# A transformer layer on one core: the second expert matrix split whole for seven experts, first rows by one-hot products, a later evacuation

## The chip, the cores and the metric

The kernel runs on one core of a Trainium2 chip. The metric is the device time in microseconds (us) of the whole program; the median of several runs is compared. The engines are TensorE (PE: matmuls; PEld its weight loads), VectorE (DVE), ScalarE (ACT), GpSimd (POOL) and SyncE (SP), each with its own queue of instructions, in which it works strictly in order; transfers run on 16 DMA engines.

## The reference

One decoder layer in fp32, 1024 tokens of width 1024: a modulated norm, one projection into the queries, keys and values of two attention kinds, the attentions, an output projection with a gated residual; then a second modulated norm, a router, and 32 experts of which each token takes four.

```
    x = x + gate1 * mixed
    h2 = rms_norm(x, norm2_g) * (1.0 + scale2) + shift2
    logits = h2 @ w_router + b_router
    top_val, top_idx = lax.top_k(logits, 4); gates = softmax(top_val)
    # for each expert e, over the rows xe that chose it:
        gu = xe @ w_gate_up[e] + b_gate_up[e]          # 1024 x 2048
        g = min(gu[:, :1024], 7);  u = clip(gu[:, 1024:], -7, 7)
        y = ((u + 1) * g * sigmoid(1.702 * g)) @ w_down[e] + b_down[e]
    return x + gate2 * sum over a token's experts of gate * y
```

An expert's two matrices are 12 MB in fp32, read once each: 384 MB in all.

## The kernel before

Four stages follow each other: the projections, the attentions, then eight row blocks of 128 tokens (output projection, norm, router), then the 32 experts.

**The row blocks** (class `Block`). Block by block the kernel computes x1 (`products`, `add`), the norm's factor (POOL takes a power, line 111, from `rsqrt_start`), the rows h2 (`rows_start`, `rows_out`, which writes them to the DRAM buffer `h2d`), the router's logits and the four choices (`logits`), each row's place within its experts (`places`), and a table row per choice: `scattered` issues four indirect DMAs on POOL, line 982, from `pay` (token and gate) to the places `sli` in the DRAM table `tab`. Before that, `places` lets POOL write the token numbers into `pay` (line 944). `pay` and `sli` come from a pool with three buffers, and the last block has its own. For the expert that is done first, the rows' list is also kept on chip: `hot` is a one-hot matrix (token by place), `tg` holds token, gate and a one, and `listed` adds hot's product with tg for each block into the PSUM tile `p0` (line 960); after the last block DVE makes the list `slots0` of it, POOL gathers the rows from `h2d` (line 1146), and PE transposes them (line 1174).

**The experts.** An order by rank is computed from the counts of rows. An expert at a position works with a fixed number of columns C, its capacity: 172, 136, 200, 128, 136, 128, 188, ... down to 96 (rows above it go through a loop at the end). Up to 128 rows are one row block, above that there are two. An expert's weights are 12 chunks of 1 MB. Ten of them are split into a high part (ACT, line 826, two halves a chunk, `hb`) and a low part in bf16 (DVE, line 813, `ha`); the activations are split likewise (`xx`, `xb`). `products` then takes four columns blocks of 128 at once: 32 matmuls of the high weights with high and low activations side by side (line 1196, max(256, 2C) columns), and 32 of the low weights with the activations in bf16 (line 1202, C columns). Chunks 8 and 9, the first half of the down matrix's columns, are not split: `expert` multiplies them as plain fp32 (line 1252, 32 matmuls that the profile shows as 64 records), from two buffers of their own (`draw`). The other chunks go through a ring of six (`eraw`).

In the plain product ACT evacuates a pair of output blocks to `yl` (line 1263) as soon as it is finished: blocks 0 and 1 before PE has done 2 and 3. The transposes of the next expert's rows (`between`, that is `stage_t`, line 1174) stand after each half of it. PSUM has four tiles of two banks in rotation (`banks`).

What starts when is written by hand: PE, ACT, DVE and SP execute in program order. `done()` is called at 14 places of an expert; the table TG says up to which of the 20 halves splits may then have been issued (`pump`), and `pump` also issues every chunk load for which a buffer is free. NH = 12 halves may be split ahead. The chunk loads stand on SP's queue, gathers and scatters on POOL's.

## Time and profile before

| | |
|---|---|
| median of 3 runs | 2157.39 us (2155.97 to 2163.31) |
| the profiled execution | 2155.82 us, span 2154.0 us |
| PE, PEld | 2046.7 us (95%), 1914.8 us (89%) |
| DVE, ACT, POOL | 1631.7 (76%), 1357.8 (63%), 481.7 us (22%) |
| DMA | 549.53 MB, mean 255 GB/s |
| first product of the first expert starts | 745.96 us |

The span runs from the first to the last instruction of the profiled execution. A share of busy time is a mean over the four stages; the section of rows below therefore cuts the span by windows. Idle time of an engine is put down to what came last of the things it waited for.

### The profile page before, as it was taken

What the parts mean: (1) busy time and instruction counts of PE and PEld (TensorE: products, weight loads), DVE (VectorE), ACT (ScalarE), POOL (GpSimd) and SP (SyncE); (2) the same over time, 40 slices, a digit from 0 to 9 for tenths busy, and PEclk for the clock granted to TensorE, in tenths of its full rate; (3) what the DMA queues carried; (4) which work ended last, traced back from release to release, by engine and by line L of the source; (5) the groups of instructions that cost most, each with busy time, mean ns of one, the idle gap of its engine ahead of it and who ended that gap; (6) DMA issues with size and microseconds to landing.
All of it is one profiled execution on the core that took longest, in us unless ns stands there. A gap on an engine that the chain in (4) does not pass through costs nothing.

```text
span 2154.0 us, 43837 instructions
## 1 busy us (share of the span) xinstructions
PE 2046.7 (95%) x16922; PEld 1914.8 (89%) x16922; DVE 1631.7 (76%) x2838; ACT 1357.8 (63%) x2391; POOL 481.7 (22%) x466
## 2 busy tenths in 40 slices
PE   6999999999999699999999999999999999999997
PEld 6877778998887599999998999999999999999996
DVE  6587765776666778788787877878878878878884
ACT  3522314777643367677677677777877777768774
POOL 2245532111013411112111222112111211211211
PEclk9999999999999799999999999999999999999998
DMA  8267886442233498899799999989999999999993
GB/s 296 67 161 220 217 237 164 112 114 70 90 129 145 158 338 293 268 337 343 268 295 347 289 315 317 324 296 349 309 321 300 355 319 330 325 332 322 332 321 81
DMA packets 273655, 549.53 MB, mean 255 GB/s; under 512 B 31796, under 2 KB 31812, under 8 KB 273316
## 3 DMA queue, kind: packets, MB, share of 16 engines
q1 hardware_dynamic: 251507, 490.61, 67.4%
q0 software_dynamic: 21936, 56.09, 11.2%
q8 instruction: 134, 2.20, 0.4%
q14 instruction: 78, 0.63, 0.1%
HBM read 501.84 MB, written 44.78 MB: 254 GB/s over the span
## 4 chain that ended last, share of the span: by engine, by line
PE 61%; ACT 5%; DMA 3%; DVE 3%; issue 2%; POOL 1%; POOLq 0%; SPq 0%; ACTq 0%; DVEq 0%
PE gu L1196 30%; PE gu L1202 13%; PE gu L1252 10%; PE gu L1285 2%; ACT hb L826 2%; PE gu L1174 2%; PE po L605 1%; ACT yl L1263 1%; DMA eraw<-in_w_down_dram 1%; DMA eraw<-in_w_gate_up_dram 1%; PE pss L567 1%; DMA tab<-pay,sli 1%; PE pt L598 1%; POOL tab L982 1%; DVE ha L813 0%
## 5 line engine op out<-in xcount | busy, mean ns | idle before, releaser
L813 DVE TENSOR_TENSOR ha<-eraw,hb 128x1024 bf16<-128x1024 f32 x640 | 760.0, 1240 | 7.7 <-ACT hb L826 7.7
L826 ACT ACTIVATE hb<-eraw 128x1024 fp32r<-128x1024 f32 x640 | 634.1, 1050 | 21.2 <-DMA eraw<-in_w_down_dram 15.3
L1196 PE MATMUL gu<-xx,hb 128*128 128x256 f32 (+13 forms) x4096 | 586.3, 299 | 2.2 <-DVE xx L1178 2.2
L1196 PEld LDWEIGHTS gu<-xx,hb 128*128 128x128 f32 x4096 | 552.9, 189 | 2.6 <-DVE xx L1178 2.4
L1202 PEld LDWEIGHTS <-ha 128*128 128x128 bf16 x5120 | 310.6, 97 | 11.8 <-issue 1.5
L1252 PE MATMUL gu<-ay,draw 128*128 128x128 f32 (+19 forms) x2048 | 277.9, 292 | 36.4 <-ACT yl L1263 32.9
L1252 PEld LDWEIGHTS gu<-ay,draw 128*128 128x128 f32 x2048 | 260.5, 192 | 44.5 <-ACT yl L1263 39.7
L1202 PE MATMUL gu<-xb,ha 128*128 128x128 bf16 (+19 forms) x4096 | 271.6, 224 | 0.0
L1216 ACT ACTIVATE tb<-gu,bcol 128x128 f32<-128x128 f32 (+19 forms) x512 | 156.9, 369 | 89.8 <-PE gu L1202 80.8
L1182 POOL DMA_INDIRECT out_dram<-y,slot x47 | 79.7, 1695 | 404.9 <-ACT y L1286 263.0
L1146 POOL DMA_INDIRECT xg<-h2d,slot x47 | 65.9, 1401 | 393.0 <-PE gu L1174 86.8
L1196 PE MATMUL gu<-ax,hb 128*128 128x256 f32 (+13 forms) x1024 | 144.5, 298 | 0.0
L1276 ACT ACTIVATE tb<-gu,bcol,g2c 128x128 f32<-128x128 f32 (+19 forms) x128 | 56.3, 465 | 132.4 <-PE gu L1202 104.8
L1196 PEld LDWEIGHTS gu<-ax,hb 128*128 128x128 f32 x1024 | 137.4, 188 | 0.6
L571 DVE CUSTOM_DVE_ANT_0 p<-pss,bias 128x1024 f32<-128x1024 f32 (+7 forms) x128 | 94.4, 755 | 52.1 <-ACT p L580 23.5
L1277 DVE SCALAR_TENSOR_TENSOR ay<-gu,g2c,tb 128x128 f32<-128x128 f32 (+19 forms) x128 | 46.2, 362 | 113.9 <-ACT tb L1276 113.9
L1258 POOL CAST ab<-ax 128x512 bf16<-128x512 f32 (+19 forms) x64 | 69.7, 1094 | 263.7 <-ACT ax L1256 263.7
L605 PE MATMUL po<-vsb,pT 128*128 128x64 f32 (+1 forms) x864 | 111.3, 275 | 2.9 <-ACT pT L599 1.4
L605 PEld LDWEIGHTS po<-vsb,pT 128*128 128x128 f32 x864 | 105.4, 194 | 5.8 <-ACT pT L599 2.0
L580 ACT ACTIVATE p<-p,mn 128x1024 f32<-128x1024 f32 (+7 forms) x128 | 98.6, 773 | 11.9 <-DVE mn L571 11.2
L111 POOL TENSOR_TENSOR rrs<-vrs,nhalf 128x8 f32<-128x8 f32 (+2 forms) x48 | 66.1, 1377 | 169.6 <-DVE vrs L109 167.8
L459 PE MATMUL pp<-wh,hb 128*128 128x512 f32 x240 | 100.5, 419 | 0.0
(275 smaller groups left out, 3080.6 us busy)
## 6 DMA issues: line engine op xcount, KB each, us to landing
eraw<-in_w_gate_up_dram SPq DMA_DIRECT2D x256, 1024.0 KB
draw<-in_w_down_dram SPq DMA_DIRECT2D x64, 1024.0 KB
eraw<-in_w_down_dram SPq DMA_DIRECT2D x64, 1024.0 KB
wraw<-in_w_ada_dram SPq DMA_DIRECT2D x32, 512.0 KB
wraw<-in_w_in_dram SPq DMA_DIRECT2D x23, 512.0 KB
hb<-in_w_ada_dram SPq DMA_DIRECT2D x16, 512.0 KB
qd<-tt POOLq DMA_DIRECT2D x32, 256.0 KB, 3.7
kd<-tt POOLq DMA_DIRECT2D x32, 256.0 KB, 4.0
```

Of the source, the lines that this page charges most:

```text
L459: nc.tensor.matmul(pp, hh[b][:, k], wh[:, kk], start=(k == 0), stop=False)
L571: nc.vector.tensor_tensor_reduce(p[:, :n], pss[:, :n], bias[:, (NB - 1 - ib) * P:(NB - 1 - ib) * P + n], -1.0, 3.0e38, OP.add, OP.min, mn)
L580: nc.scalar.activation(p, p, AF.Exp, bias=self.mn[c], scale=-1.0, accum_out=self.l[:, c:c + 1])
L605: nc.tensor.matmul(self.po[:, :w], self.pT[:, k], vsb[self.br][:, k, self.h * w:(self.h + 1) * w], start=(k == 0), stop=(k == self.ib))
L813: nc.vector.tensor_tensor(parts[t][1], raws[c][:, 2 * q:2 * q + 2], parts[t][0].bitcast(F32), OP.subtract)
L826: nc.scalar.activation(h_, raws[c][:, 2 * q:2 * q + 2], AF.Copy)
L1182: nc.gpsimd.indirect_dma_start(out=out, out_offset=bass.IndirectOffsetOnAxis(ap=sl.bitcast(I32)[:n, 0:1], axis=0), in_=y[:n], in_offset=No ...
L1196: nc.tensor.matmul(pg[j // 2][:, j % 2, :max(256, 2 * C)], w[k][0][:, j * P:(j + 1) * P], xk[k], start=(k == 0), stop=False)
L1202: nc.tensor.matmul(pg[j // 2][:, j % 2, C:2 * C], w[k][1][:, j * P:(j + 1) * P], xb[:, k], start=False, stop=(k == KT - 1))
L1216: nc.scalar.activation(t[:, j], p[:, j, C:2 * C], AF.Identity, bias=bc[:, f + j:f + j + 1], scale=1.0)
L1252: nc.tensor.matmul(place(j), raw[:, k, j * P:(j + 1) * P], a[:, 4 * kh + k], start=(kh + k + j % 2 == 0), stop=(kh == 1 and k == 3 and j % ...
L1258: nc.gpsimd.tensor_copy(ab[:, f], ah[:, f, :C].bitcast(F32))
```

## The change

Constants CWH = 164 and a second table TGW of twelve entries are new. The parts:

- **Whole split.** The seven experts with C of 164 or more (172, 200, 188, 180, 172, 168, 164, at positions 0, 2, 6, 10, 14, 18, 22) split chunks 8 and 9 too; all their 12 chunks go through the ring of six, 24 halves. In place of the plain product stands a third kind of call of `products`, with the two halves of the next rows' transposes in its middle (`mid`), and the evacuation of the split products (`outgoing`). Their activations are split by two column blocks (`activations(f, 2)`), after each pair of `a`, instead of by four.
- **Late evacuation.** In the other 25 experts (`plain`) the four yl activations stand behind all 32 matmuls.
- **First rows.** The list of the first expert from blocks 0 to 6 is read after the last block's `add`, and the rows gathered then, into `hb` buffers. The last block's rows don't go through DRAM for this expert: `stage_0` multiplies the gathered rows by the identity and adds the product of the last block's h2 with its one-hot matrix. `listed` of the last block, its list, the order by counts and what hangs on it come after that. Rows of the list that belong to the last block point to zeroed rows of `h2d` in the early gather (one DMA more, in the attention stage).
- **pay and sli** have a buffer for each of the eight blocks.
- The count of overflowing rows is read into registers at position 5 instead of after the last expert.

```diff
+CWH = 164
+TGW = (12, 14, 16, 18, 19, 21, 23, 24, 26, 30, 31, 36)
...
+                nc.sync.dma_start(h2d[S - P:S, :], z)
...
+            whole = [CAPS[r] >= CWH for r in seq]
+            splits = [(i * NCH + c, q) for i in range(E) for c in range(NCH) if whole[i] or c not in PLAIN for q in range(2)]
...
-                return "p" if d % NCH in PLAIN else "s"
+                return "p" if d % NCH in PLAIN and not whole[d // NCH] else "s"
...
-                    pay = (sm if self.b < NB - 1 else rt).tile([P, TOPK, 2], F32, name="pay")
+                    pay = rt.tile([P, TOPK, 2], F32, name="pay", bufs=NB)
...
-                    self.sli = (sm if self.b < NB - 1 else rt).tile([P, TOPK], I32, name="sli")
+                    self.sli = rt.tile([P, TOPK], I32, name="sli", bufs=NB)
...
-            cur.add(1)
-            pv.listed()
+            early = [rt.tile([P, 2], F32, name=f"early{i}") for i in range(len(BLOCKS0))]
+
+            def fetch_list():
+                nc.vector.tensor_copy(sums0, p0[:, :3 * len(BLOCKS0)])
+                slots_of(sums0, early)
+
+            cur.add(1, fetch_list)
+            xg0 = []
+            for (t0, n), sl in zip(BLOCKS0, early):
+                xg0.append(slot(False).bitcast(F32))
+                nc.gpsimd.indirect_dma_start(out=xg0[-1][:n], out_offset=None, in_=h2d,
+                                             in_offset=bass.IndirectOffsetOnAxis(ap=sl.bitcast(I32)[:n, 0:1], axis=0))
...
+        def stage_0(st):
+
+            st["x"] = operand(C0, "xx", "xb")
+            bc = st["bc"]
+            nc.vector.tensor_mul(bc[:, 2 * KT:], bc[:, 2 * KT:], g2c)
+            pts = [banks().rearrange("p g (k c) -> p (g k) c", k=4) for _ in BLOCKS0]
+            for (t0, n), xg, pt in zip(BLOCKS0, xg0, pts):
+                for k in range(KT):
+                    nc.tensor.matmul(pt[:, k, :n], xg[:n, k * P:(k + 1) * P], ident[:n, :n], start=(k % 4 == 0), stop=False)
+            for (t0, n), pt in zip(BLOCKS0, pts):
+                for k in range(KT):
+                    nc.tensor.matmul(pt[:, k, :n], cur.h2[:, k * P:(k + 1) * P], cur.hot[:, t0:t0 + n],
+                                     start=False, stop=(k % 4 == 3))
+                operand_of(st, t0, n, pt)
...
-                    for k in range(4 * kh, 4 * kh + 4):
-                        nc.tensor.matmul(pg[j // 2][:, j % 2, :max(256, 2 * C)], w[k][0][:, j * P:(j + 1) * P], xk[k],
-                                         start=(k == 0), stop=False)
+                for j, k in [(j, 4 * kh + q + r) for q in ((0, 2) if kh and mid else (0,)) for j in range(4)
+                             for r in range(2 if kh and mid else 4)]:
+                    nc.tensor.matmul(pg[j // 2][:, j % 2, :max(256, 2 * C)], w[k][0][:, j * P:(j + 1) * P], xk[k],
+                                     start=(k == 0), stop=False)
                 if kh == 0:
                     done(high=2)
+                    if mid:
+                        low_products(range(4), range(4))
+                        mid()
+            low_products(range(4), range(4 if mid else 0, KT))
...
+        def plain(C, a, bc, d0, activations, between):
...
+                    if j == 1:
+                        activations(4 * kh, 4)
+                        done()
+                if kh:
+                    yl = ap_.tile([P, 4, C], F32, name="yl")
+                    for f in range(4):
+                        nc.scalar.activation(yl[:, f], place(f), AF.Identity,
+                                             bias=bc[:, 2 * KT + f:2 * KT + f + 1], scale=g2c[:, f:f + 1])
...
+                    if whole[i]:
+                        activations(f, 2)
...
-                    if kh and j % 2:
-                        if j == 1:
-                            yl = ap_.tile([P, 4, C], F32, name="yl")
-                        for f in (j - 1, j):
-                            nc.scalar.activation(yl[:, f], place(f), AF.Identity,
-                                                 bias=bc[:, 2 * KT + f:2 * KT + f + 1], scale=g2c[:, f:f + 1])
...
+            if whole[i]:
+                pg = products(C, s_a, t0 + 16, lambda: (between(0), between(1)))
+                yl = ap_.tile([P, 4, C], F32, name="yl")
+                outgoing(yl, pg, 0)
+                done(high=2, low=4)
+            else:
+                yl = plain(C, a, bc, d0, activations, between)
+            pg = products(C, s_a, t0 + (20 if whole[i] else 16))
...
-        st = stage_g(0)
+        st = {"C": C0, "bc": cols.pop(0), "blocks": BLOCKS0, "slots": slots.pop(0)}
+        stage_0(st)
         cur.scattered()
-        stage_t(st, 0)
-        stage_t(st, 1)
...
+            if i == 5:
+                n_over = nc.values_load(tot[0:1, 0:1], min_val=0, max_val=P)
```

Where instructions move, the order of each engine shows it (what an instruction waits for stands in brackets; DMAHW and DMASW are transfers). On PE, the second half of the plain product of the second expert, before: `xg` are the next expert's rows, `ax` the split activations.

```order
L1252 MATMUL gu<-ay,draw 128x136 [waits DMAHW7_49,DVE_49]
L1252 MATMUL gu<-ay,draw 128x136
L1252 MATMUL gu<-ay,draw 128x136 [waits DVE_49]
L1252 MATMUL gu<-ay,draw 128x136 x5
L1252 MATMUL gu<-ay,draw 128x136 [waits Activation_49]
L1252 MATMUL gu<-ay,draw 128x136 x7
L1174 MATMUL gu<-ident,xg 128x128 x4
L1174 MATMUL gu<-ident,xg 128x72 x4
L1196 MATMUL gu<-ax,hb 128x272 [waits DVE_49,PE_49]
```

And the same place after; the plain product's line is now 1241, the transposes' 1171, the split product's 1220.

```order
L1241 MATMUL gu<-ay,draw 128x136 [waits DMAHW0_49,DVE_49]
L1241 MATMUL gu<-ay,draw 128x136
L1241 MATMUL gu<-ay,draw 128x136 [waits DVE_49]
L1241 MATMUL gu<-ay,draw 128x136 x13
L1171 MATMUL gu<-ident,xg 128x128 x4
L1171 MATMUL gu<-ident,xg 128x72 x4
L1220 MATMUL gu<-ax,hb 128x272 [waits DVE_49,PE_49]
```

The wait for ACT within the plain product is gone; the 16 matmuls stand in the same order. On PE ahead of the first expert, before: `tg` and `hot` make the list (line 960), line 1072 counts rows for the order, line 1174 transposes the gathered rows.

```order
L940 MATMUL po<-msk,upper 128x32 [waits DVE_49]
L941 MATMUL po<-mcum,ones 128x32
L960 MATMUL p_6067<-tg,hot 128x3 [waits DVE_49,Pool_49]
L960 MATMUL p_6067<-tg,hot 128x3
L1072 MATMUL po<-mcum,ones 128x32 [waits DVE_49]
L1174 MATMUL gu<-ident,xg 128x128 [waits DMASW2_49,PE_49]
L1174 MATMUL gu<-ident,xg 128x128 x3
L1174 MATMUL gu<-ident,xg 128x44 [waits DMASW3_49,DVE_49]
L1174 MATMUL gu<-ident,xg 128x44 x3
L1174 MATMUL gu<-ident,xg 128x128 x4
L1174 MATMUL gu<-ident,xg 128x44 x4
L1196 MATMUL gu<-xx,hb 128x344 [waits DVE_49]
```

And after; line 1190 multiplies the gathered rows (in `hb` buffers) by the identity, line 1193 the last block's rows by its one-hot matrix.

```order
L954 MATMUL po<-msk,upper 128x32 [waits DVE_49]
L955 MATMUL po<-mcum,ones 128x32
L1190 MATMUL gu<-ident,hb 128x128 [waits DMASW6_49,PE_49]
L1190 MATMUL gu<-ident,hb 128x128 x7
L1190 MATMUL gu<-ident,hb 128x44 [waits DMASW7_49,DVE_49]
L1190 MATMUL gu<-ident,hb 128x44 x7
L1193 MATMUL gu<-hb 128x128 x8
L1193 MATMUL gu<-hb 128x44 x8
L1394 MATMUL gu<-tg,hb 128x3 x2
L1402 MATMUL gu<-mcum,ones 128x32 [waits DVE_49,PE_49]
L1220 MATMUL gu<-xx,hb 128x344 [waits DVE_49]
```

The transposes have become two sets of sixteen matmuls, the list's product and the row count have moved behind them, and the transfers that PE waits for are the early gathers. On POOL around the last block, before: line 111 is the power of the norm, line 982 the table scatters, line 1146 the first expert's gathers.

```order
L982 DMA tab<-pay,sli 36864x2 x4
L111 TENSOR_TENSOR rr_7253<-vr_7251,nhalf 128x1
L982 DMA tab<-pay,sli 36864x2 x4
L111 TENSOR_TENSOR rr_7418<-vr_7416,nhalf 128x1
L982 DMA tab<-pay,sli 36864x2 x4
L1146 DMA xg<-h2d,slots_2975 128x1024
L1146 DMA xg<-h2d,slots_2976 44x1024
L982 DMA tab<-pay,sli 36864x2 x4
L1179 CAST xb<-xx 128x8x128
```

And after; the power is line 113, the scatters line 990, the gathers line 1074.

```order
L990 DMA tab<-pay,sli 36864x2 x4
L113 TENSOR_TENSOR rr_7255<-vr_7253,nhalf 128x1
L990 DMA tab<-pay,sli 36864x2 x4
L1074 DMA hb<-h2d,early_7413 128x1024
L113 TENSOR_TENSOR rr_7429<-vr_7427,nhalf 128x1
L1074 DMA hb<-h2d,early_7414 44x1024
L990 DMA tab<-pay,sli 36864x2 x8
L1180 CAST xb<-xx 128x8x128
L1180 CAST xb<-xx 128x8x44
```

The first gather now stands ahead of the last block's power and the second behind it, both ahead of the last two blocks' scatters.

## Rows read from the trace of the kernel before

**Rows 1.** Windows: length, busy of PE PEld DVE ACT POOL, granted clock, DMA share, GB/s.
```profile
600.00:733.60 133.60, 120.12 (x643) 100.38 (x641) 86.33 (x275) 49.56 (x153) 42.98 (x58) 0.93 0.36 130
733.60:746.00 12.40, 3.77 (x19) 2.73 (x19) 6.50 (x23) 2.80 (x4) 7.04 (x7) 0.50 0.59 191
745.90:1140.00 394.10, 385.73 (x3543) 377.81 (x3544) 315.49 (x452) 279.92 (x439) 67.53 (x56) 1.00 0.91 305
1140.00:2100.00 960.00, 932.79 (x9079) 913.47 (x9078) 788.40 (x1043) 716.16 (x1143) 188.16 (x169) 1.00 0.97 322
```

**Rows 2.** The page, part 5: the lines named in the text.
```profile
L813 DVE TENSOR_TENSOR ha<-eraw,hb 128x1024 bf16<-128x1024 f32 x640 | 760.0, 1240 | 7.7 <-ACT hb L826 7.7
L826 ACT ACTIVATE hb<-eraw 128x1024 fp32r<-128x1024 f32 x640 | 634.1, 1050 | 21.2 <-DMA eraw<-in_w_down_dram 15.3
...
L1252 PE MATMUL gu<-ay,draw 128*128 128x128 f32 (+19 forms) x2048 | 277.9, 292 | 36.4 <-ACT yl L1263 32.9
...
L1277 DVE SCALAR_TENSOR_TENSOR ay<-gu,g2c,tb 128x128 f32<-128x128 f32 (+19 forms) x128 | 46.2, 362 | 113.9 <-ACT tb L1276 113.9
```

**Rows 3.** Waits of PE, 745 to 2130 us: total, times, longest.
```profile
PE gu L1252 <- ACT yl L1263: 32.1, 31, 3.2
```

**Rows 4.** Timeline of PE, second expert: start, length, line, what it waited for.
```profile
830.67 2.12 PE L1252 MATMUL gu<-ay,draw 128*128 128x136 f32 x16 [0.91 <-ACT yl L1263]
832.63 0.85 PE L1174 MATMUL gu<-ident,xg 128*128 128x128 f32 x8
833.28 4.27 PE L1196 MATMUL gu<-ax,hb 128*128 128x272 f32 x32
```

**Rows 5.** Chain of waits, first expert (172 columns): start, length, what.
```profile
770.27 5.10 PE gu L1196 x32
775.37 2.42 PE gu L1202 x32
777.79 4.71 PE gu L1252 x32
...
785.84 0.89 ACT yl L1263 x2
```

**Rows 6.** Chain of waits, third expert (200 columns).
```profile
867.14 5.88 PE gu L1196 x32
873.02 2.76 PE gu L1202 x32
875.78 5.44 PE gu L1252 x32
```

**Rows 7.** Windows, the first expert.
```profile
746.00:797.80 51.80, 50.83 (x401) 49.57 (x402) 40.60 (x48) 34.47 (x52) 10.13 (x8) 0.97 0.93 332
```

**Rows 8.** Waits of all engines, 600 to 735 us.
```profile
POOL pay L944 <- DMA tab<-pay,sli: 10.5, 4, 3.2
...
PE p L960 <- DVE tg L955: 6.2, 5, 2.3
```

**Rows 9.** Timeline of PE ahead of the first expert.
```profile
729.13 0.99 PE L960 MATMUL p<-tg,hot 128*128 128x3 f32 x4 [1.20 <-DVE tg L955]
...
738.03 1.08 PE L1174 MATMUL gu<-ident,xg 128*128 128x128 f32 x4 [4.04 <-DMA xg<-h2d,slots]
741.49 2.25 PE L1174 MATMUL gu<-ident,xg 44*128 44x44 f32 x12 [2.37 <-DMA xg<-h2d,slots]
745.96 1.51 PE L1196 MATMUL gu<-xx,hb 128*128 128x344 f32 x4 [2.22 <-DVE xx L1178]
```

**Rows 10.** Timeline of POOL, the same stretch.
```profile
722.44 0.57 POOL L111 TENSOR_TENSOR rr<-vr,nhalf 128x1 f32<-128x1 f32 x1 [2.17 <-DVE vr L109]
...
732.27 1.02 POOL L1146 DMA_INDIRECT xg<-h2d,slots  x1 [2.11 <-DMA h2d<-h]
733.60 1.66 POOL L1146 DMA_INDIRECT xg<-h2d,slots  x1 [0.31 <-DVE mcum L978]
```

**Rows 11.** Chain of waits, ninth expert.
```profile
1116.45 20.55 DMA eraw<-in_w_down_dram
```

More of the change, by code (lines that the diff above doesn't have):

```diff
@@ L145, in hybrid_layer @@
     PLAIN = (8, 9)
-    SPLIT = [c for c in range(NCH) if c not in PLAIN]
-    NSP = 2 * len(SPLIT)
     tmp.close()
@@ L820, in split_half @@
                 t = at_["split"]
-                c, q = chunk_of(t)
+                c, q = splits[t]
                 h_ = slot(False).rearrange("p (k n) -> p k n", k=2)
@@ L829, in split_half @@
                 at_["split"] += 1
-                if t == E * NSP - 1:
+                if t == len(splits) - 1:
                     low(t)
@@ L1191, in products, with low_products @@
             w = [tuple(q[:, j] for q in parts[t]) for t in range(t0, t0 + 4) for j in range(2)]
-            assert t0 + 3 < at_["split"] - 1 or at_["split"] == E * NSP
+            assert t0 + 3 < at_["split"] - 1 or at_["split"] == len(splits)
+            def low_products(js, ks):
+                for j in js:
+                    for k in ks:
+                        nc.tensor.matmul(pg[j // 2][:, j % 2, C:2 * C], w[k][1][:, j * P:(j + 1) * P], xb[:, k],
+                                         start=False, stop=(k == KT - 1))
@@ L1198, in products @@
                 if kh == 0:
                     done(high=2)
-            for j in range(4):
-                for k in range(KT):
-                    nc.tensor.matmul(pg[j // 2][:, j % 2, C:2 * C], w[k][1][:, j * P:(j + 1) * P], xb[:, k],
-                                     start=False, stop=(k == KT - 1))
-            return pg
+                    if mid:
+                        low_products(range(4), range(4))
+                        mid()
+            low_products(range(4), range(4 if mid else 0, KT))
@@ new lines, in products, with place @@
+            return pg
+        def plain(C, a, bc, d0, activations, between):
+            pg = banks()
+            def place(j):
+                return pg[:, j // 2, j % 2 * 256:j % 2 * 256 + C]
+            for kh in range(2):
+                raw = raws.pop(d0 + kh)
+                for j in range(4):
+                    for k in range(4):
+                        nc.tensor.matmul(place(j), raw[:, k, j * P:(j + 1) * P], a[:, 4 * kh + k],
+                                         start=(kh + k + j % 2 == 0), stop=(kh == 1 and k == 3 and j % 2 == 1))
+                    if j == 1:
[6 more added lines that the diff above has]
+                                             bias=bc[:, 2 * KT + f:2 * KT + f + 1], scale=g2c[:, f:f + 1])
+                freed["p"] += 1
+                done()
+                between(kh)
+            return yl
```

149 lines of the change are left out of this document (73 added, 76 removed).

## The prediction

> **What bounds the kernel now.** I read the windows first, then the waits of TensorE (PE), and last the chain of waits. In the windows [rows 1] the experts' stretch is 1354 us of the 2154.0 us span, and PE is busy for 98% of its first part (385.73 of 394.10) and 97% of its second (932.79 of 960), at the full clock. So a microsecond of PE work or of PE waiting that disappears there is worth up to a microsecond. The same rows hold the warning: the DMA engines' share is 0.91 before 1140 us and 0.97 after it. Weights stream all through the experts, and in the second part only 0.03 of 960, some 29 us, is free on the DMA side. The two earlier stretches look different: 600 to 733.6 us has PE busy 120 of 133.6 us, and in the 12.4 us ahead of the first expert PE works 3.77 us at a granted clock of 0.50, with DMA at 0.59: a stretch of pure latency.
>
> PE's waits inside the experts are nearly one line: L1252 for ACT's yl, 32.1 us in 31 places [rows 3]. The timeline shows one: 0.91 us before the last 16 records of L1252 [rows 4]; the order before has the wait at exactly that matmul. One of the 31 is 3.2 us long; the other thirty average 28.9/30 = 0.96 us, the value used below.
>
> **Late evacuation.** The order after has no ACT wait within the plain product. Thirty waits of 0.96 us, one for the long one and a last one of that kind [the page counts 32.9 in all, rows 2] make about 30 us; I count 31 × 0.96 = 29.8. What hides the evacuation then is PE's next work: eight transposes (0.85 us, rows 4) and the next product's first tile. Four yl activations are 2 × 0.89 = 1.8 us on ACT [rows 5]. The next product uses two of four bank pairs; when the expert after has two row blocks its second tile falls on the plain product's pair and must wait for yl. That tile comes after the transposes and 8 matmuls of 4.27/32 = 0.13 us [rows 4], 1.9 us in all, so the wait is nil when ACT is free and up to one split (1.05 us, rows 2) when one stands ahead in ACT's order. It can happen in 15 of the 25 plain experts: 0 to 16 us. I take 0.25 us each, 4 us, because ACT is busy 716 of 960 us [rows 1] and often isn't free. Sum of this part: 25.8.
>
> **The whole split.** Seven experts replace 64 plain records by a product. At 172 columns a plain half of 32 records is 4.71 us, so 9.42 the pair, and a product is 5.10 + 2.42 = 7.52: 1.90 saved [rows 5]. At 200 columns it is 2 × 5.44 = 10.88 against 5.88 + 2.76 = 8.64: 2.24 [rows 6]. On the straight line between them 188, 180, 168 and 164 columns save 2.09, 2.00, 1.85 and 1.80, so all seven save 1.90 × 2 + 2.24 + 2.09 + 2.00 + 1.85 + 1.80 = 13.8 us of PE. The price stands on other engines: four more splits per such expert, 4 × 1.24 = 5.0 us of DVE and 4 × 1.05 = 4.2 us of ACT [rows 2], and four more of L1277's evacuations on DVE, 4 × 0.36 = 1.4 us [rows 2]. The first expert keeps DVE busy 40.6 of 51.8 us [rows 7]; after, it is about 47 of 48.9. ACT goes from 34.5 to 39. DVE thus just fits, with nothing to spare, and the two raw buffers of the plain chunks stand empty there, so the stream looks two chunks less far ahead.
>
> **Routing blocks.** POOL waits 10.5 us, four times, for the landing of the table scatter before it may overwrite pay [rows 8]; behind that wait stand its power (L111, the rows' norm), then DVE's tg, then PE's list matmul. PE's waits for tg are 6.2 us in five places [rows 8]; one, 1.20 us, belongs to the last block [rows 9], which leaves 5.0. With a buffer for each block the POOL wait goes. What is late next is DVE, busy 86 of 133.6 us [rows 1]; so 4.5, bounds 0 to 5.
>
> **First rows.** Before, the two gathers start at 732.27 and 733.60 [rows 10], their rows let PE go on at 738.03 and 741.49, and PE starts the first product at 745.96 [rows 9]. After, the gathers need only blocks 0 to 6; in POOL's order the first stands ahead of the last block's power, the second just behind, and that power ran at 722.44 [rows 10], so I put their starts some 8 us earlier, near 724 and 726. The last block's rows come by one-hot products that need its hot tile, read by PE at 729.13 [rows 9]. No trace row has these products. Sixteen matmuls give 32 records behind hot. The nearest row is the plain half: at 172 columns 4.71/32 = 0.147 us a record at the full clock [rows 5]. These have 128 or 44 columns in equal number, 86 on average and so half of that, and run at a clock of 0.50, so double: 0.147 again, 4.7 us in all. The lower bound is the transposes beside them, 3.33 us for 16 [rows 9]. If the gathered rows are in by 729, PE ends these at 729.1 + 4.7 = 733.8, and 2.2 us later, as now from 743.74 to 745.96 [rows 9], the product starts: 736 to 737, a gain of 9. If they land late, 7.8 us after issue as the last gather now (733.60 to 741.36), the other 16 matmuls are still ahead: up to 743 to 744.5, a gain of 1.5. POOL's power also waits behind a gather's 1.0 to 1.7 us [rows 10], which moves hot back by as much. I take 740, a gain of 6. The order and count arithmetic that moves behind this, some 20 small DVE instructions, hides beside the first products, and if it doesn't it delays their splits by its 4 to 5 us at most.
>
> In the row the transposes take 1.08 and 2.25 us, 3.33 for 16 [rows 9], less than any estimate for the products. The Trainium skill ("Perfetto Trace Analysis", Transposes) says that logical transposes should use transpose and not a standard matmul, because a transpose skips arithmetic. By that rule alone this part would cost 2 × 4.7 − 3.3 = 6 us on PE and gain nothing. The rows put the latency of the gathers, 4.04 and 2.37 us of PE's waiting, and not PE, on the path, so I follow them; the gain of 1.5 above is the low end of this part.
>
> The moved count read at the end and the extra zeroing in the attention stage I cost at nothing: the first lies beside the last scatter, the second beside attention's idle queues; without that cover each is one small DMA, a few tenths.
>
> **The stream.** PE terms: 25.8 + 13.8 + 4.5 + 6 = 50.1 us. Bytes are unchanged, so the DMA share must rise. Before 1140 us there are 0.09 × 394 = 35 us free against a PE gain there of 9 × 0.96 + 1.90 + 2.24 + 2.09 less 1.25 of bank waits = 13.6; I take 2 as lost. From 1140 to 2100 PE would gain 22 × 0.96 + 7.65 less 2.75 = 26 us, and only 29 are free. A ring of six chunks can't use all of them: already now one wait for a chunk spans 20.55 us of the chain [rows 11], and ACT idled 15.3 us for down chunks [rows 2]. I take 16 of the 26, a loss of 10. So 50.1 − 12 = 38 us. Against the profiled run's 2155.82 (span 2154.0) that gives 2118; the median of the runs shown, 2157.39, is 1.6 higher, and I put it at 2119.
>
> **Rivals.** *The stream keeps up.* Then all of 50 us is gained: 2107. For it: the first expert's window moved 332 GB/s at a share of 0.93 [rows 7]. Against: that later share, and the waits for chunks [rows 2, 11]. The second part's row has 322 GB/s at a share of 0.97 [rows 1]. The Trainium skill ("Perfetto Trace Analysis", Roofline) gives 358 GB/s as a core's share of the memory and about 120% of it as the practical ceiling for a core alone; by this the stream has a quarter more in it and the time would be this rival's 2107. The trace shows no stretch here near that.
>
> *The stream binds from 1140 on.* Nothing of the 26 is gained: 50 − 26 = 24, so 2133. For it: the share of 0.97 there; against: the 29 us still free.
>
> *The yl wait moves.* Each of the 15 experts waits 0.96 again at the next product's second tile, ten more than I took; with less pressure on the stream the gain is 31: 2126.
>
> *The whole experts run dry (slower).* Two chunks less ahead is 2 × 1.05 MB at 322 GB/s [rows 1], about 6.5 us, and with DVE full nothing catches it up. Paid in each of seven it is 46 us: 50 − 46 − 12 = −8, 2165. It turns slower from (50 − 12)/7 = 5.4 us per whole expert. Against it: the DMA share of the early whole experts is 0.93 [rows 7], and the ring's six buffers stay.
>
> *The front doesn't move*: routing and first rows give nothing, 38 − 10.5 = 27.5, 2130.
>
> **The numbers.** Forecast 0.50 (own range 2111 to 2128), keeps up 0.17, binds 0.14, yl moves 0.08, front 0.06, run dry 0.05. The range for eight in ten is 2104 to 2138. This kernel's measurement can't tell less than 0.3%, 6.5 us: faster is below 2150.9, slower above 2163.9. Only the dry case and tails of binding get there: faster 0.91, same 0.05, slower 0.04.
>
> **What would show it.** In the profile after: no wait of the plain product for yl, under 8 us of waits of products for yl; in the seven whole experts a product in place of L1252 and each 2.8 us shorter in all; DVE above 93% in the first; PE's first product near 740 less the 4.5 gained ahead of it; DMA share from 1140 on at 0.99 or more, with 8 to 15 us more of PE or ACT waits for chunks. The forecast is wrong if these waits stay as they were (then near 2107) or if PE waits for splits over 5 us in each whole expert.

## The result and the profile after

The changed kernel takes 2129.84 us (median of 4 runs, 2126.65 to 2134.75), the kernel before 2158.26 us on the same chip: a ratio of 0.9867, 95% interval 0.984 to 0.9894, or 28 us less. On another chip, in the experiments below, the same pair gave 0.9899 (0.987 to 0.9927). The profiled execution has a span of 2132.9 us, 21 less than before; it was the slowest of the four runs.

The page's busy times and the lines that answer to [rows 2] (busy us and mean ns; idle us before them and what ended it):

```profile
PE 2042.7 (96%) x16970; PEld 1908.1 (89%) x16970; DVE 1681.3 (79%) x2914; ACT 1382.7 (65%) x2433; POOL 504.9 (24%) x480
...
L825 DVE TENSOR_TENSOR ha<-eraw,hb 128x1024 bf16<-128x1024 f32 x668 | 796.5, 1248 | 5.8 <-ACT hb L838 5.8
L838 ACT ACTIVATE hb<-eraw 128x1024 fp32r<-128x1024 f32 x668 | 659.8, 1050 | 25.8 <-DMA eraw<-in_w_down_dram 23.6
...
L1241 PE MATMUL gu<-ay,draw 128*128 128x128 f32 (+13 forms) x1600 | 200.0, 283 | 6.9 <-DVE ay L1296 6.0
```

PE is busy 4 us less than before. The experts' products (L1220, L1214 and L1241; before, L1196, L1202 and L1252) take 1338.8 us where they took 1348.2, and the output projection 4.2 us less; against that stand 13.3 us for the first rows' products where transposes took 3.3 [rows 9]. DVE has 28 splits more and is busy 50 us more. L1241, the plain product, has lost its wait for yl altogether.

The first product starts at 736.46 instead of 745.96 us [rows 9]. PE's timeline there (start, length, line, tiles, count):

```profile
721.64 0.61 PE L955 MATMUL po<-mcum,ones 128*128 128x32 f32 x2
722.07 7.33 PE L1190 MATMUL gu<-ident,hb 128*128 128x128 f32 x32
729.33 6.02 PE L1193 MATMUL gu<-hb 128*128 128x128 f32 x32
...
736.46 6.85 PE L1220 MATMUL gu<-xx,hb 128*128 128x344 f32 x32 [0.45 <-DVE xx L1179]
```

So 9.5 of the span's 21 us come ahead of the experts and only 11.6 in them: from the first product to PE's last instruction it was 1395.0 us and is 1383.4. PE's waits there (total us, times, longest), which before were 32 us of yl [rows 3] and 5.5 of others:

```profile
PE gu L1220 <- DVE xx L1179: 6.4, 9, 1.9
PE gu L1241 <- DVE ay L1296: 6.0, 6, 2.1
PE gu L1328 <- DVE ay L1307: 5.4, 10, 1.4
PE gu L1214 <- POOL ab L1268: 4.6, 3, 2.1
PE gu L1171 <- DVE su L1276: 3.0, 2, 1.9
PE gu L1220 <- ACT y L1329: 2.7, 7, 0.6
```

Sorting the experts by kind shows where. In the sum of their lengths, from one expert's first product to the next's, the seven whole experts went from 361.6 to 359.2 us, the seven behind them from 281.1 to 290.1, and the eighteen others from 752.3 to 734.1. The others gained 18 us; the whole ones, each with 1.9 less to multiply and no yl wait, gained almost nothing, and those behind them lost 9.

The windows of the first four experts (whole, behind, whole, behind; columns as in [rows 1]), to be held against [rows 7]:

```profile
736.50:790.90 54.40, 51.45 (x400) 49.76 (x401) 47.42 (x79) 37.76 (x57) 11.38 (x10) 0.91 0.72 250
790.90:832.90 42.00, 41.24 (x418) 40.20 (x417) 37.79 (x50) 33.77 (x54) 9.51 (x7) 1.00 1.04 366
832.90:888.50 55.60, 54.74 (x413) 52.99 (x410) 47.94 (x107) 37.29 (x56) 11.53 (x9) 1.00 0.69 221
888.50:930.40 41.90, 40.19 (x420) 38.75 (x417) 37.84 (x51) 33.12 (x54) 9.14 (x7) 1.00 1.04 369
```

DVE is busy 47.4 of 54.4 us and 47.9 of 55.6 in the whole experts. The DMA engines run at a share of 0.72 and 0.69 there, and at 1.04 with 366 and 369 GB/s behind them. PE's timeline in the middle of the first whole expert, and DVE's at that place:

```profile
768.08 2.77 PE L1220 MATMUL gu<-ax,hb 128*128 128x344 f32 x16
770.69 1.38 PE L1214 MATMUL gu<-ab,ha 128*128 128x172 bf16 x16
773.10 0.66 PE L1171 MATMUL gu<-ident,xg 128*128 128x128 f32 x4 [1.03 <-DVE su L1276]
775.68 2.16 PE L1171 MATMUL gu<-ident,xg 8*128 8x8 f32 x12 [1.92 <-DVE su L1276]
777.76 4.64 PE L1220 MATMUL gu<-ax,hb 128*128 128x344 f32 x16
```

```profile
767.99 4.62 DVE L825 TENSOR_TENSOR ha<-eraw,hb 128x1024 bf16<-128x1024 f32 x4
772.54 0.50 DVE L1276 SCALAR_TENSOR_TENSOR su<-tb,gu 128x344 f32<-128x344 f32 x1
```

The next rows' transposes (L1171) need the PSUM tile of the product that ended at 768; its evacuation (L1276) stands behind four splits on DVE and starts at 772.54. PE waits 1.03 and 1.92 us. And the 16 matmuls of L1220 that took 2.77 us before the wait take 4.64 after it. The granted clock in windows around it shows why:

```profile
765.00:772.00 7.00, 7.00 (x70) 6.61 (x68) 6.16 (x8) 5.44 (x8) 0.00 (x0) 1.00 0.86 298
772.00:775.00 3.00, 0.72 (x5) 0.42 (x4) 2.38 (x5) 1.00 (x3) 0.45 (x1) 1.00 0.97 346
775.00:777.70 2.70, 2.02 (x12) 1.67 (x12) 2.01 (x6) 1.19 (x3) 0.48 (x2) 0.51 1.05 365
777.70:782.20 4.50, 4.50 (x18) 4.39 (x17) 4.50 (x5) 3.23 (x5) 4.29 (x4) 0.54 0.42 120
782.20:788.00 5.80, 5.80 (x47) 5.76 (x46) 3.67 (x8) 3.95 (x7) 1.15 (x2) 1.00 0.69 247
```

PE worked 0.72 of 3 us from 772, and the clock then stood at about half, the lower level of 1.2 GHz, until some 782.

### The profile page after: what moved, and what is told of

The parts are those of the page before. It is cut to its first block, busy times and chain, and to the rows that moved or that the text cites. A ratio compares the mean times of both kernels' runs of the same rounds, so it can differ in the third digit from the quotient of the medians.

```text
span 2132.9 us, 44076 instructions
## 1 busy us (share of the span) xinstructions
PE 2042.7 (96%) x16970; PEld 1908.1 (89%) x16970; DVE 1681.3 (79%) x2914; ACT 1382.7 (65%) x2433; POOL 504.9 (24%) x480
## 5 line engine op out<-in xcount | busy, mean ns | idle before, releaser
L825 DVE TENSOR_TENSOR ha<-eraw,hb 128x1024 bf16<-128x1024 f32 x668 | 796.5, 1248 | 5.8 <-ACT hb L838 5.8
L838 ACT ACTIVATE hb<-eraw 128x1024 fp32r<-128x1024 f32 x668 | 659.8, 1050 | 25.8 <-DMA eraw<-in_w_down_dram 23.6
L1220 PE MATMUL gu<-xx,hb 128*128 128x256 f32 (+13 forms) x4096 | 587.2, 300 | 6.3 <-DVE xx L1179 3.6
L1220 PEld LDWEIGHTS gu<-xx,hb 128*128 128x128 f32 x4096 | 553.6, 189 | 8.9 <-DVE xx L1179 4.7
L1214 PEld LDWEIGHTS <-ha 128*128 128x128 bf16 x5344 | 328.3, 98 | 18.7 <-issue 6.9
L1214 PE MATMUL gu<-xb,ha 128*128 128x128 bf16 (+19 forms) x4096 | 271.6, 224 | 0.0
L1241 PE MATMUL gu<-ay,draw 128*128 128x128 f32 (+13 forms) x1600 | 200.0, 283 | 6.9 <-DVE ay L1296 6.0
L1241 PEld LDWEIGHTS gu<-ay,draw 128*128 128x128 f32 x1600 | 191.6, 192 | 8.9 <-DVE ay L1296 7.3
L1220 PE MATMUL gu<-ax,hb 128*128 128x256 f32 (+13 forms) x1248 | 190.7, 309 | 5.3 <-DVE xx L1179 2.8
L1220 PEld LDWEIGHTS gu<-ax,hb 128*128 128x128 f32 x1248 | 177.7, 192 | 8.1 <-DVE xx L1179 3.4
L1268 POOL CAST ab<-ax 128x344 bf16<-128x344 f32 (+19 forms) x78 | 70.8, 908 | 368.1 <-ACT ax L1266 368.1
L1305 ACT ACTIVATE tb<-gu,bcol,g2c 128x172 f32<-128x172 f32 (+19 forms) x156 | 69.4, 470 | 115.1 <-PE gu L1214 66.2
L581 ACT ACTIVATE p<-p,mn 128x1024 f32<-128x1024 f32 (+7 forms) x128 | 98.6, 773 | 14.2 <-DVE mn L572 13.8
L600 ACT ACTIVATE pT<-pt 128x512 f32<-128x512 f32 (+3 forms) x144 | 65.0, 486 | 52.9 <-PE pt L599 52.1
L462 PE MATMUL pp<-wl,hb 128*128 128x512 f32 x240 | 95.0, 396 | 0.0
```

What stands on the lines that cost most here:

```text
L462: nc.tensor.matmul(pp, hh[b][:, k], wl[:, kk], start=False, stop=(k == KT - 1))
L581: nc.scalar.activation(p, p, AF.Exp, bias=self.mn[c], scale=-1.0, accum_out=self.l[:, c:c + 1])
L825: nc.vector.tensor_tensor(parts[t][1], raws[c][:, 2 * q:2 * q + 2], parts[t][0].bitcast(F32), OP.subtract)
L838: nc.scalar.activation(h_, raws[c][:, 2 * q:2 * q + 2], AF.Copy)
L1214: nc.tensor.matmul(pg[j // 2][:, j % 2, C:2 * C], w[k][1][:, j * P:(j + 1) * P], xb[:, k], start=False, stop=(k == KT - 1))
L1220: nc.tensor.matmul(pg[j // 2][:, j % 2, :max(256, 2 * C)], w[k][0][:, j * P:(j + 1) * P], xk[k], start=(k == 0), stop=False)
```

## The experiments

Each ratio is to the kernel before, run beside it on the same chip; its median was 2152.3 to 2155.2 us there. Theory W, formed from the profile above: in the whole experts DVE's and ACT's in-order queues are too full, PE waits, and the whole split costs more than it saves. Its rival, S, was my prediction's own term: the weights' stream binds.

**The whole split undone.**

```diff
-CWH = 164
+CWH = 999
```

> The changed kernel without the whole split: no expert has a capacity over the bound (CWH 999), so all 32 take the plain product; late evacuation, first rows and buffers stay. Theory W (in the seven whole experts the extra splits stand in DVE's order ahead of evacuations, PE waits for PSUM there and in the next expert, and the ring runs the DMA engines idle): the 18 plain experts without such a neighbour already save about 1.16 us each in the trace, so 32 x 1.16 = 37 plus 9.5 ahead of the experts: 2158 - 46.5 = about 2111, faster than the changed kernel's 2130. Theory S (the weights' stream binds everywhere, whatever DVE does): the 13.8 us of PE work come back and the stream gives nothing: 2136 to 2142.

Measured: 2109.14 us, ratio 0.9803 (0.9781 to 0.9825). W's 2111 was met; S's 2136 to 2142 is out. The whole experts' places take 352.8 us in sum (359.2 with the split), those behind 273.1 (290.1). All seven behind are shorter, but of the whole ones' places only four are. The third, the seventh and the eleventh expert are longer without the split: 56.59 us (with it 55.54), 52.78 (50.70) and 50.67 (49.36). So the split did save time in three whole experts, less than their followers lost. The same kernel once more, beside a later experiment:

> The kernel of e1_no_whole again, on the chip of e9_no_low, for a comparison at one place: 0.980 of the kernel before by both theories.

Measured: 2106.32 us, 0.978 (0.9762 to 0.9798). Its windows of the same four experts and of a long stretch, and the PE waits of over 0.5 us in sum in the experts' stretch:

```profile
735.10:784.00 48.90, 48.90 (x401) 47.84 (x401) 43.62 (x71) 34.45 (x52) 10.48 (x8) 1.00 0.87 316
784.00:824.60 40.60, 40.60 (x419) 40.16 (x417) 35.38 (x48) 32.69 (x52) 7.80 (x7) 1.00 1.02 345
824.60:881.20 56.60, 56.60 (x413) 55.47 (x410) 44.00 (x99) 34.56 (x52) 10.30 (x7) 1.00 0.85 283
881.20:920.40 39.20, 39.20 (x419) 38.61 (x417) 34.38 (x47) 31.92 (x52) 8.52 (x7) 1.00 0.88 291
1120.00:2055.00 935.00, 928.50 (x9094) 912.03 (x9094) 789.73 (x1043) 711.17 (x1140) 196.53 (x170) 1.00 0.99 331
```

```profile
PE gu L1241 <- DVE ay L1296: 3.5, 6, 1.0
PE gu L1220 <- DVE xx L1179: 2.6, 5, 0.8
PE gu L1220 <- DVE ax L1267: 0.7, 1, 0.7
```

PE is busy in every microsecond of the first four experts, at the full clock, and 928.5 of 935 later, with the DMA share at 0.99: PE hardly waits for the stream even there. The experts' products take 1338.6 us of PE here, and 1338.8 in the changed kernel: in that profile, nothing was left of what the split saves PE.

**Late evacuation alone**, in the kernel before:

```diff
-                    if kh and j % 2:
-                        if j == 1:
-                            yl = ap_.tile([P, 4, C], F32, name="yl")
-                        for f in (j - 1, j):
-                            nc.scalar.activation(yl[:, f], place(f), ...)
...
+                if kh:
+                    yl = ap_.tile([P, 4, C], F32, name="yl")
+                    for f in range(4):
+                        nc.scalar.activation(yl[:, f], place(f), ...)
```

> The kernel before with one edit: the four yl evacuations stand behind all matmuls of the plain product. Theory W: all 32 experts get about 1.16 us shorter, 2158 - 37 = 2121, that is more than the whole change gives. Theory S: the stream takes half of it back, about 2138.

Measured: 2120.56 us, 0.9855 (0.9832 to 0.9878), 31 us. This one edit gives as much as the whole change. The experts' stretch is 1361.2 us (1395.0 before), 33.8 less for 32.1 us of yl waits that went.

**The front alone** (no whole split, yl evacuated early as before):

> The changed kernel without whole split and with the yl evacuations as before: the first rows, the buffers of pay and sli and the early count remain. The first product starts 9.5 us earlier in the changed kernel's profile. If all of that stays to the end: 2149. If the order of the experts, which is known later now (DVE ends it at 740.5, the first loads of the second expert wait for it), costs the first expert time: 2151 to 2154.

Measured: 2138.05 us, 0.9931 (0.9909 to 0.9953), 14.8 us: more than any case I gave, and the later order of the experts costs nothing, since the first expert is no longer than before (51.6 us).

**The buffers of pay and sli alone**, in the kernel before:

```diff
-pay = (sm if self.b < NB - 1 else rt).tile([P, TOPK, 2], F32, name="pay")
+pay = rt.tile([P, TOPK, 2], F32, name="pay", bufs=NB)
-self.sli = (sm if self.b < NB - 1 else rt).tile([P, TOPK], I32, name="sli")
+self.sli = rt.tile([P, TOPK], I32, name="sli", bufs=NB)
```

> The kernel before with pay and sli in a buffer for each block, nothing else. By the prediction's term: 4.5 us less, 2154. Rival: DVE is late next and the gain is under 1 us: 2157 to 2158.

Measured: 2144.02 us, 0.9961 (0.9949 to 0.9974), 8.8 us by the medians. Of the waits of [rows 8], POOL's for the scatter's landing is gone, and PE's for tg is left with 1.5 of 6.2 us:

```profile
POOL tab L982 <- DVE lg L920: 39.6, 6, 7.0
...
PE p L960 <- DVE tg L955: 1.5, 3, 1.2
```

From the start of the first to the start of the last matmul of the output projection it is 126.2 us, where it was 133.2. Of these 7.0 us, 2.9 are idle time of PE and 4.1 busy time. Before, a stretch at the lower clock followed a wait of 1.41 us for tg, shown here (columns as in [rows 1]); in this run the granted clock is 1.00 throughout:

```profile
694.80:701.60 6.80, 6.80 (x28) 6.11 (x28) 4.77 (x11) 2.46 (x7) 0.17 (x2) 0.50 0.19 77
```

The first rows then make 14.8 − 8.8 = 6 us by the medians, with intervals that leave some 1 to 12 us. The traces say more. From the first matmul of the output projection to the first product it is 159.8 us before, 152.6 with the buffers alone and 146.4 in the front alone. But ten profiles here have these products, and only in three of them is it that short (145.9 to 147.3); in the other seven, the changed kernel's among them, it is 149.2 to 150.6. So the first rows give 2 to 3.4 us in seven executions and 5.3 to 6.7 in three; they differ in the granted clock of this stretch, as the last experiment shows.

**Why the whole split costs: DVE's load.** The extra low halves on POOL:

```diff
+                eng = nc.gpsimd if c % NCH in PLAIN else nc.vector
-                nc.vector.tensor_tensor(parts[t][1], ...)
+                eng.tensor_tensor(parts[t][1], ...)
```

> The changed kernel with one edit: in the seven whole experts the four low halves of chunks 8 and 9 are subtracted on POOL instead of DVE. Theory W (DVE's full, in-order queue is what PE waits for): 4 x 1.24 = 5 us less for DVE in each whole expert; most of what the whole split lost comes back, 7 to 15 us faster than the changed kernel on the same chip. Rival R (the two raw buffers taken from the chunk stream are the cause, the DMA engines idle at a share of 0.69 to 0.79 in those experts for that reason): DVE's relief changes nothing, within 3 us, or it gets slower if POOL is late with the low half.

Measured: 2150.52 us, 0.9979 (0.9965 to 0.9993), 15 us slower than the changed kernel beside it. It doesn't decide between W and R; R's last clause (slower if POOL is late) may fit too. A half takes POOL 3.0 us, and DVE's own halves got longer, 1293 ns where they were 1248:

```profile
L826 DVE TENSOR_TENSOR ha<-eraw,hb 128x1024 bf16<-128x1024 f32 x640 | 792.9, 1293 | 8.4 <-ACT hb L839 8.4
...
L826 POOL TENSOR_TENSOR ha<-eraw,hb 128x1024 bf16<-128x1024 f32 x28 | 83.3, 3002 | 0.9 <-ACT hb L839 0.5
```

**The two raw buffers given back** to the stream:

```diff
-                return "p" if d % NCH in PLAIN and not whole[d // NCH] else "s"
+                return "p" if d % NCH in PLAIN else "s"
...
-                    freed["s"] += 1
+                    freed[kind_of(c)] += 1
```

> The changed kernel with one edit: chunks 8 and 9 of the whole experts go through the two buffers of the plain chunks, as in the other experts, instead of the ring of six, and are split from there. Rival R: the stream is two chunks further ahead again and 7 us or more come back. Theory W: DVE's work is the same, the gain is 0 to 4 us.

Measured: 2139.95 us, 0.9918 (0.9887 to 0.995), no better than the changed kernel beside it. Its first whole expert and the one behind:

```profile
735.20:789.90 54.70, 50.75 (x401) 48.92 (x401) 48.71 (x79) 37.92 (x57) 11.31 (x10) 0.93 0.71 251
789.90:831.70 41.80, 41.31 (x421) 40.29 (x418) 37.58 (x50) 33.63 (x53) 9.38 (x7) 1.00 1.04 369
```

The share of the DMA engines there is as low as without the buffers (0.72 and 1.04), so it isn't for want of buffers that the loads start late. Rival R is out. What ends most of SP's waits for a buffer is a low half on DVE (919 us over the experts, 955 in the changed kernel beside it); that these come late because DVE's queue is full is read from the traces, not tested alone.

> The changed kernel itself, on the same chip as the two before it, so that they are compared at one place; 0.9867 of the kernel before was measured. Both theories: the same within 0.3%.

Measured: 2135.24 us, 0.9899 (0.987 to 0.9927), the control for the two above; the 0.9867 of the first measurement lies just below this interval, though the two intervals overlap.

**DVE's load taken away, not moved.** PE multiplies a constant where the low halves of chunks 8 and 9 would stand (the kernel leaves them out of its result, so only its time is of use):

```diff
-                parts[t] = h_, pair[-1][:, t % 2]
+                parts[t] = h_, (None if c % NCH in PLAIN else pair[-1][:, t % 2])
...
-                        ... w[k][1][:, j * P:(j + 1) * P], xb[:, k],
+                        ... ident.bitcast(BF16)[:, :P] if w[k][1] is None else w[k][1][:, j * P:(j + 1) * P], xb[:, k],
```

> The changed kernel with the four low halves of chunks 8 and 9 in the seven whole experts left out: their weights' low part isn't computed, PE multiplies a constant tile in its place, so PE, ACT and the loads do what they did and only DVE has 5 us less in each of these experts (the output differs by that). Theory W (DVE's work in its order is what PE waits for): most of the waits in the whole experts and the experts behind them go; at best the whole split's 13.8 us become a gain over the kernel without it, ratio 0.974 to 0.983, at least half of the distance from the changed kernel's 0.990 back to e1_no_whole's 0.980. Rival Q (the whole experts lose by something else that comes with the split: the ring's gating of the loads, ACT's four splits more, the transposes in the middle of a product): 0.987 to 0.991 as before.

Measured: 2125.02 us, 0.9863 (0.9843 to 0.9883), beside 0.978 for the kernel without the whole split. The ratio misses W's range (0.974 to 0.983) and Q's 0.987 lies within its interval, so W in this form is half right at most: the whole experts fall to 350.3 us (356.8 in the control), but those behind stay at 291.1 (291.8). What they wait for is still there (L1329 is L1328 of the changed kernel):

```profile
PE gu L1329 <- DVE ay L1308: 6.3, 11, 1.4
```

L1329 transposes the results of the expert before; they wait for its last evacuation, and ahead of that stand five splits on both ACT and DVE.

**The burst moved** behind the last evacuation:

```diff
-TGW = (12, 14, 16, 18, 19, 21, 23, 24, 26, 30, 31, 36)
+TGW = (12, 14, 16, 18, 19, 21, 23, 24, 26, 28, 29, 36)
```

> The changed kernel with two entries of TGW lower (28, 29 in place of 30, 31): between the two evacuations of the second matrix stand 3 splits in place of 5 on DVE and ACT, and 7 in place of 5 after the last one. In e9_no_low the seven experts behind the whole ones stayed as long as in the changed kernel (291.1 us in sum, 291.8; without the whole split 273.2), with PE waiting for the last evacuation. Theory B (the burst of splits ahead of the last evacuation is what the followers wait for): 2 x 1.24 = 2.5 us earlier each, the followers' sum falls by 9 to 16 us, ratio 0.983 to 0.986 where the changed kernel has 0.987 to 0.990. Rival L (DVE and ACT are full in these experts, and a split moved back is only waited for later): within 3 us of the changed kernel.

Measured: 2130.72 us, 0.9889 (0.987 to 0.9909): no gain beside the changed kernel's 0.9867 and 0.9899 on other chips, as rival L had it. The wait for the last evacuation is gone and another has taken its place: the products' second pair of PSUM tiles waits for ACT's y, the next instruction behind the splits that were moved. The total over the experts' stretch, then ACT and PE behind the third expert:

```profile
PE gu L1220 <- ACT y L1329: 14.2, 7, 2.3
```

```profile
889.02 6.73 ACT L838 ACTIVATE hb<-eraw 128x1024 fp32r<-128x1024 f32 x7
895.65 2.10 ACT L1329 ACTIVATE y<-gu,slot 128x1024 f32<-128x1024 f32 x2
```

```profile
892.88 1.96 PE L1214 MATMUL gu<-xb,ha 128*128 128x128 bf16 x32
896.80 3.56 PE L1220 MATMUL gu<-xx,hb 128*128 128x256 f32 x20 [1.96 <-ACT y L1329]
```

Seven splits in a row are 6.73 us on ACT, and PE waits 1.96 us for what stands behind them; in the changed kernel this wait was 2.7 us in sum. The experts behind the whole ones grew to 297.5 us.

> The table of e11_table together with the edit of e9_no_low: the low halves of chunks 8 and 9 in the whole experts aren't computed, a constant stands in their place. Theory B: both gains add, ratio about 0.978, at the level of the kernel without the whole split. Rival L: DVE has 5 us of room in each whole expert here, so what is moved back isn't waited for: the table helps here even if it doesn't in e11_table, 0.978 to 0.982. If neither explains it: 0.986 as e9_no_low.

Measured: 2129.35 us, 0.9881 (0.9859 to 0.9903). With DVE's load lightened too, the experts behind stay at 296.5 us, which neither B nor L expected. So what holds them is not DVE's sum of work. PE waits for ACT's y 14.3 us there, behind the seven splits, as in the run before: the wait stands wherever the burst stands, which speaks for the order. A whole expert's 24 halves are issued at 12 places where others issue 20 at 14, and at some places that means five or seven at once. ACT's sum of work, four splits more in each whole expert, was not made lighter in any run; it stays a rival.

**First rows by transposes** (without the whole split):

```diff
-nc.tensor.matmul(pt[:, k, :n], xg[:n, ...], ident[:n, :n], start=(k % 4 == 0), stop=False)
+nc.tensor.matmul(pt[:, k, :n], xg[:n, ...], ident[:n, :n], start=(k % 4 == 0), stop=False, is_transpose=True)
```

> The changed kernel without the whole split (as e1_no_whole), and with the gathered first rows put into PSUM by PE's transpose mode instead of by products with the identity; the last block's one-hot products still add to them. In the profile of e1_no_whole the 32 records of the identity products take 5.89 us with PE never waiting. If PE is the path there: 16 transposes of about 0.2 us, 3.3 us, so the first product starts 2 to 3.5 us sooner after the last block's choice, and the ratio is 0.001 to 0.0016 lower than e1_no_whole's 0.9803. If the gathers' landing or the hot tile is late next: within 1 us.

Measured: 2103.59 us, 0.9757 (0.9728 to 0.9786), the fastest kernel here. Its profile, and the one of the first no-whole run:

```profile
723.70 1.95 PE L1190 MATMUL gu<-ident,hb 128*128 128x128 f32 x8
726.25 1.08 PE L1190 MATMUL gu<-ident,hb 44*128 44x44 f32 x8 [0.60 <-DVE pos L980]
727.26 5.61 PE L1193 MATMUL gu<-hb 128*128 128x128 f32 x32
...
733.98 6.84 PE L1220 MATMUL gu<-xx,hb 128*128 128x344 f32 x32 [0.45 <-issue]
```

```profile
719.91 5.89 PE L1190 MATMUL gu<-ident,hb 128*128 128x128 f32 x32
725.72 3.77 PE L1193 MATMUL gu<-hb 128*128 128x128 f32 x32
...
730.63 6.84 PE L1220 MATMUL gu<-xx,hb 128*128 128x344 f32 x32 [0.47 <-issue]
```

The first part fell from 5.89 to 3.6 us, but the one-hot products behind it took 5.61 instead of 3.77, so the first product starts 10.3 us after the first part's start here and 10.7 there: 0.4 us. The two profiles were at different clocks, though. The granted clock was 0.50 in the first part and 0.65 in the second here, 0.64 and 1.00 there. The second no-whole run is the same kernel as the first, at 0.50 and 0.59:

```profile
720.59 7.33 PE L1190 MATMUL gu<-ident,hb 128*128 128x128 f32 x32
727.85 6.12 PE L1193 MATMUL gu<-hb 128*128 128x128 f32 x32
```

There the first product starts 14.5 us after the first part's start, so against this profile the transposes are worth 4.2 us, and 3.7 in the first part at the same clock. One kernel thus differs by 3.8 us between two executions, more than the edit was expected to give, and one profile each can't tell what it is worth. The timed ratio lies within the intervals of the kernel without the edit.

## Why the prediction was right, and where it wasn't

The sign and the range held: 28 us gained, 38 forecast, 2129.84 in 2104 to 2138. That the range held is in part luck. The forecast's own range, 2111 to 2128, was missed; the time is that of the rival *the front doesn't move* (2130), though the front did move, by 9.5 us. Two kinds of terms were wrong in opposite directions: the whole split lost some 37 us against the sum, and the evacuation, the buffers and the stream gave some 21 more than summed.

Of the signs I had named, the yl wait went, the first product came at 736.46 (735.5 was said) and ACT's waits for down chunks grew by 8 us. But the whole experts became 0.3 us shorter each on average and not 2.8, DVE was busy 87% of the first and not 93, and the DMA share from 1140 us on was 0.96 and not 0.99. PE is idle 3.3 us on average in a whole expert and the one behind it together; the 5 us that I had called a sign of being wrong were too high a bar, since the loss was larger than the waits.

- **Late evacuation**, 25.8 forecast: 31 measured alone. The wait goes as the order said, and the wait that I put in its place, at the next product's second tile (4 us, and the rival of 14), doesn't come: without the whole split PE never waits for yl. Each wait also cost more than its 0.96 us: experts that don't wait for anything else got shorter by 1.1 to 1.2 (40.38 to 39.25 us in the tenth, with a wait of 0.89). The records of two groups of matmuls that follow without a wait overlap (in [rows 4] 830.67 + 2.12 ends 0.16 us after 832.63); at a wait that overlap is lost too, which would account for most of the rest.
- **Routing blocks**, 4.5 forecast: 8.8 measured, 7.0 of it in the row blocks. PE's waits for tg fell by 4.7, while those for nm (L940) grew from 3.2 to 4.8; the rest is 4.1 us less of busy time, as the 6.8 us at the lower clock went. The term was short in part because it counted the waits and not the clock behind them.
- **First rows**, 6 forecast: 6 by the difference of two medians, 2 to 3.4 us or 5.3 to 6.7 by the traces. That 6 came out is luck. The gathers were in before PE wanted them, so PE was the path. Then both sets of products have to be paid behind the last block's counts (L955), as the order after shows, and not the one set that I charged. The price was off as well. The first set took 5.9 to 7.3 us and the second 3.8 to 7.1, against 4.7 each: at the full clock 32 records of 128 or 44 columns took 3.77 us, 0.118 each, where I had halved 0.147 for having half the columns. The rule weighed there (the Trainium skill, "Perfetto Trace Analysis", Transposes) has it that a logical transpose should not be a standard matmul; the traces agree that transposes are shorter, 3.6 against 7.3 us at a clock of 0.50, but not with my reading that this part would then gain nothing.
- **The whole split**, 13.8 forecast as a gain: a loss. This is the step that failed: "DVE thus just fits". The PE side was right to the tenth: the one whole expert without a wait, the seventh, is 50.70 us against 52.78 with the plain product, 2.08 less, 2.09 forecast. But I added up DVE's busy time and not its order. Whole experts and those behind them took 359.2 + 290.1 us, without the split 352.8 + 273.1: 23.4 lost where 13.8 were to be won, together 37 us or 5.3 for each whole expert and its follower. (The 7.65 in the stream's sum should be 7.55; it changes nothing.) By the timed runs the loss is 14 us (0.9867 against 0.9803) to 26 us (0.9899 against 0.978).
- **The stream**, 12 us of loss forecast: about none without the whole split, where PE was busy 928.5 of 935 us, and none for the late evacuation alone, whose waits came through whole. I read a share of 0.97 as a ceiling; behind the whole experts the same engines move 366 to 369 GB/s at 1.04, against 322. The rival *the stream keeps up* had this right. The ceiling that I took from the Trainium skill ("Perfetto Trace Analysis", Roofline), about 120% of 358 GB/s for a core alone, isn't contradicted: 369 GB/s is the most in the windows shown, and no run here shows a ceiling. As an estimate from that page it is a third above 322 GB/s, not a quarter.
- The rival *the whole experts run dry* named the right place and nearly the right price (6.5 us for each whole expert, slower than before from 5.4 on; 5.3 were measured), and the wrong cause: two more buffers changed nothing. The kernel didn't come out slower because the evacuation, the buffers and the stream gave 5, 4 and 12 us more than I had summed.

Shown is that the whole split loses, that DVE's load is a part of it (6.5 us in the whole experts), that buffers are not, and that behind the whole experts PE waits for what stands behind a burst of splits, in both tables that were run. That a finer spread of the splits would save it was not tried.

How the loss divides can be read from the changed kernel's trace, held against the second run without the split (351.3 + 273.1 us, with PE never idle in those 14 experts). PE is idle 11.9 us in the whole experts and 11.2 behind them. In the whole experts it is also busy 9.8 us longer than that run's busy time less 13.8; the granted clock is at the lower level for 17.1 us there (10.2 of them in the first expert), which would make some 8.5, an estimate at half speed. Behind them the granted clock is 1.00 throughout, and still PE is busy 5.8 us longer: in the fourth expert four waits of 1.70 us in all make it 2.7 us longer, some 0.25 us for each wait beyond its own length, as in the tenth expert above.

## What to carry to other kernels

Moving work off the bounding engine is only free if the engines that take it have room in order, at the places where something is waited for: look at what stands ahead of each evacuation, not at their sum of busy time. Time each part of a change alone; here one part of four took back a third to a half of what the others gave, and one moved evacuation equalled the whole. Look at the clock of a stretch before one profile is held against another: the same kernel's differed by 3.8 us in one place. A wait taken away at a saturated engine can be worth more than its length, and a DMA share near 1 is no proof of a bound.

## What the hardware showed that I had not expected

- Behind two waits of 1.03 and 1.92 us, with PE at work for 0.72 of 3 us, the granted clock was 0.51 and 0.54 for some 7 us, and 16 matmuls took 4.64 instead of 2.77 us. In the row blocks before, a wait of 1.41 us stood ahead of 6.8 us at 0.50. So a wait of 1 to 2 us in a full stretch can cost as much again; most of the waits here were not followed by a lower clock.
- At a share of 1.04 the 16 DMA engines moved 366 to 369 GB/s, at 0.99 331: the share didn't say how much more there was.
- A low half of 128 x 1024 took POOL 3.0 us and DVE 1.25, and DVE's own halves took 4% longer, 1293 ns, in the kernel in which POOL did some of them.
- The same two sets of products ahead of the first expert took 5.89 + 3.77 us in one execution of a kernel and 7.33 + 6.12 in another, at granted clocks of 0.64 and 1.00 against 0.50 and 0.59.
